# Hybrid SSD and GLA trunk on one core: sums of A beside the last scan, three kinds of work in the source's order, the meta state a piece apart

## The chip, the cores and the metric

The kernel runs on one core of a Trainium2 chip. The metric is the time of one execution on the device in microseconds, taken as the median of several runs. The engines are TensorE (PE: matrix products), VectorE (DVE) and GpSimd (POOL) for elementwise work, ScalarE (ACT: activations, copies, and a second queue of transfers) and SyncE (SP), whose queue issues most transfers and executes them in order: an issue that waits for a free tile holds all issues behind it.

## The reference, cut to what matters

One layer of a decoder trunk over 16 meta tokens and 2048 real ones, width 1024, all in float32:

```
u = rmsnorm(h, norm_w)
z, xbc, dt, q, k, v, g_gla, a_lr, merge_g = split(u @ w_in)
y_ssd = rmsnorm(ssd(silu(conv(xbc)), softplus(dt)) * silu(z))       # Mamba-2, 4 groups, chunks of 128
y_gla = rmsnorm(gla(q, k, v, log_sigmoid(a_lr @ w2 + b) / 16)) * silu(g_gla)   # 4 heads, chunks of 64
merged = sum over the two branches of sigmoid(merge_g) * (y @ w_branch)
out = rmsnorm(h + merged @ w_out, final_norm_w), without the meta tokens
```

Both scans carry a state from chunk to chunk and start from the state that the 16 meta tokens leave. The SSD scan multiplies its scores by decays exp(seg), seg being the difference of two running sums.

## The kernel before, in words

**Arithmetic.** Each fp32 operand is split into a high and a low half (ACT copies to the high half, DVE or POOL subtracts to get the low one), and `accum` (L185, L186, L187) makes each product of three matmuls.

**First phase.** The 2064 tokens go in four blocks of 512 (`BLK`); block 0 has the 16 meta tokens as well (`m0`). A block has eight units, four SSD (`ssd_proj`, `ssd_scan`) and four GLA (`gla_proj`, `gla_scan`). All of these are generators; `step()` advances the running ones by a piece after each piece of the projections, so that scans run a unit behind. Block 0 loads raw weights (`wr`, 3 tiles), splits them (L165 on ACT, L166 on POOL, into `whl`, 4 tiles) and saves the split ones by SP (L181); later blocks load those (L161). Beside the projections there run:

- `late_constants` (L332 on): the GLA gate's second matrix `gw2` in three loads (L335), its split, the masks (L339). It is called once, at the start of unit 1 of block 0.
- `fetch_u(b+1)` from unit 4 on: for each of four chunks the sum of squares of the rows of x (`rows_rstd`: two loads L258 and two squares L259, in `acc` tiles, of which there are two and which the convolution of the projections uses as well), then the normed columns (L294 loads, DVE and ACT form and split `u`).
- `beside_unit`: the differences of B that a Strassen product needs (`make_sums`: loads L76, POOL subtracts L80, stores from ACT's queue L83).

In `ssd_scan`, `before(c)` makes scores and decays of a chunk (L552: four Relu per chunk on ACT; then Exp L554, L555 masks on DVE), `after(c)` uses them (L564, L565 with the state `s_ssd`); `meta_state()` (L508 to L519) makes the state of the meta tokens first. `g_all` (L437) is the copy of a gate projection out of PSUM.

**Second phase.** Seven stages follow (gate, branch 0 and branch 1 for each half of the tokens, then out), each a 7-product Strassen form with products taken in the order 1, 2, 6, 7, 5, 3, 4. A `Stage` loads and splits B (`load_b` L884, `prep_b` L889 on ACT and L890 on DVE), loads A (`load_a` L896), makes its sums on POOL (`sum_a` L905 to L908), splits A (`prep_a` L914 on ACT, L915 on DVE, into a ring `aops` of 7) and multiplies (`product`). Products 1 and 2 need no sums of A; 6, 7, 5 and 3 do.

**The transition.** The table `between` does the first loads, splits and four early products (`NEARLY`; pairs 0 and 1, products 1 and 2) of the first gate stage beside the steps k = 0 to 8 of the last GLA scan, which ends with transposes (L803). Then the pools of the first phase are closed, new ones opened, and `run(-1)` does what the table `todo` has ahead of the next product.

**What sets the order.** In the first phase PE and SP run in the source's order; ACT, DVE and POOL run in the order of a scheduler's own simulation. In the stages only SP is held to the source's order.

Of the kernel before, what the change touches and what calls it, by code (L numbers as in the profile page):

```python
# [14 lines left out]
P = 128  # L15
# [25 lines left out]
def trunk_kernel(ctx: ExitStack, tc: tile.TileContext, xm, xmt, w_feat, w_tok, w_zm, w_br, w_o,  # L41
# [29 lines left out]

    def make_sums(pool, tag, nb, braw, sums, j, c, store):
        cs = slice(c * HB, (c + 1) * HB)
        pair = [mk(pool, [P, 512], F32, tag, bufs=nb).rearrange("p (i c) -> p i c", i=2) for _ in range(2)]
        for r, (k, t) in zip((t[:, i] for t in pair for i in range(2)), ((0, 1), (0, 0), (1, 1), (1, 0))):
            nc.sync.dma_start(r, braw(4 * k + j, t)[:, cs])  # L76
        yield
        (b12, b11), (b22, b21) = [(t[:, 0], t[:, 1]) for t in pair]
        for o, x, y in ((b11, b12, b11), (b12, b22, b12), (b22, b22, b11), (b21, b21, b22)):
            nc.gpsimd.tensor_tensor(o, x, y, op=ALU.subtract)  # L80
        yield
        for dst, src in zip(sums, pair):
            store.dma_start(dst[j][:, :, cs], src)  # L83

# [136 lines left out]
    def halves_of(pool, tag):  # L221

        bks = [bank(pool, tag) for _ in range(2)]
        return bks, [(i // 2, bks[i // 2][:, i % 2 * 256:(i % 2 + 1) * 256]) for i in range(4)]

    def rstd_of(ssq, n, scale):
        r = mk(sm, [P, 4], F32, "rstd")
        nc.vector.tensor_scalar(r[:, :n], ssq, scale, EPS, op0=ALU.mult, op1=ALU.add)
        nc.gpsimd.tensor_tensor(r[:, :n], r[:, :n], mhalf[:, :n], op=ALU.pow)
        return r  # L230
# [6 lines left out]
    def load_u(b):  # L237
# [6 lines left out]
        def rows_rstd(r0, n, vector=False):  # L244
# [9 lines left out]
            else:  # L254
                s2 = mk(sm, [P, 2], F32, "ss2")
                for i in range(2):
                    xt = mk(wk, [P, META + BLK], F32, "acc")[:, :BLK]
                    nc.sync.dma_start(xt, xm[r0:r0 + n, i * BLK:(i + 1) * BLK])  # L258
                    nc.scalar.activation(xt, xt, AF.Square, accum_out=s2[:, i:i + 1])  # L259
                nc.vector.tensor_tensor(ss, s2[:, 0:1], s2[:, 1:2], op=ALU.add)  # L260
# [6 lines left out]
        if m0:  # L267
            rm_s = rows_rstd(0, META, True)
        for c in range(NCH):
            rs.append(rows_rstd(META + b * BLK + c * P, P, c % 2))  # L270
            yield
# [15 lines left out]
        else:  # L287
# [3 lines left out]
            yield  # L291
        for kt in range(KT):
            xk = mk(wk, [P, META + BLK], F32, "act" if m0 else "acc", bufs=NACT if m0 else 2)[:, :tt]
            nc.sync.dma_start(xk, xmt[:, kt, row0:row0 + tt])  # L294
            for ps, a, n in rbs:
                nc.vector.scalar_tensor_tensor(xk[:, a:a + n], xk[:, a:a + n], norm_w[:, kt:kt + 1], ps[:, :n],
                                               op0=ALU.mult, op1=ALU.mult)
            nc.scalar.activation(uh[:, kt, :tt], xk, AF.Copy)
            nc.scalar.dma_start(u_left[b][kt], xk[:, m0:])
            nc.vector.tensor_tensor(ul[:, kt, :tt], xk, uh[:, kt, :tt].bitcast(F32), op=ALU.subtract)  # L300
            yield
        return uh, ul
# [29 lines left out]
    def late_constants():  # L332
        w2r = mk(wk, [P, META + BLK], F32, "acc")[:48, :512]
        for i in range(3):
# [159 lines left out]
    def ssd_scan(o, g, feats, zs):  # L494
# [37 lines left out]
        def before(c):  # L532
# [18 lines left out]
            for h in range(4):  # L551
                nc.scalar.activation(dm[:, h], cb[:, h], AF.Relu, scale=-1.0,  # L552
                                     bias=tkc[:, ci, 4 * g + h:4 * g + h + 1])
            nc.scalar.activation(dm, dm, AF.Exp, scale=-1.0)  # L554
            nc.vector.tensor_tensor(dm, dm, scm[:, c].unsqueeze(1).to_broadcast([P, 4, P]), op=ALU.mult)  # L555
# [27 lines left out]
        if m0:  # L583
            meta_state()
        for c in range(1, NCH):
            before(c)
            after(c - 1)
            yield
# [233 lines left out]
    def beside_unit(key):  # L822
        for j in range(4):
            for c in range(2):
                yield from make_sums(wpool, "wr", NWR, *sums[key], j, c, nc.scalar)
                yield
# [3 lines left out]
    for b in range(nblk):  # L830
        o = new_block(b, next_u[b])
        for i in range(SG + GH):
            if (b, i) in beside:
                begin(beside_unit(beside[b, i]))
            if (b, i) == (0, 1):
                late_constants()
            if i == 1:
                begin(gates(o))
            if i == SG and b + 1 < nblk:
                begin(fetch_u(b + 1))  # L840
            for _ in ssd_proj(o, i) if i < SG else gla_proj(o, i - SG):
                step()
        save(0)

# [16 lines left out]
    rpl = pool2("raws", 1)  # L861
    apl = pool2("aops", 7)
    
# [6 lines left out]
    class Stage:  # L870
# [8 lines left out]
        def load_b(self, p, j):  # L879
            src = {1: lambda j: self.braw(j, 0), 2: lambda j: self.braw(4 + j, 0), 3: lambda j: self.braw(4 + j, 1),  # L880
                   4: lambda j: self.sums[1][j][:, 1], 5: lambda j: self.sums[0][j][:, 1],
                   6: lambda j: self.sums[1][j][:, 0], 7: lambda j: self.sums[0][j][:, 0]}[p]
            raw = self.braws[p, j] = mk(rpl, [P, BLK], F32, "br", bufs=5)
            nc.sync.dma_start(raw, src(j))  # L884
# [33 lines left out]
        def product(self, n, p, early=False):  # L918
# [10 lines left out]
            if p in (1, 6, 5):  # L929
                sn = mk(rpl, [P, BLK], F32, "br", bufs=5) if early else mk(opl, [P, BLK], F32, "sn", bufs=6)  # L930
                nc.scalar.activation(sn, ps, AF.Copy)  # L931
                self.snap[n, p] = sn
# [60 lines left out]
    def out_stage():  # L993
        fns, res, ssq = [], {}, {}

        def fetch(n, i, t):
# [3 lines left out]
            if t and len(fns) < 2:  # L1000
                for hf in range(2):
                    fns.append(mk(rpl, [P, BLK], F32, "br", bufs=5))
                    nc.sync.dma_start(fns[hf], fnw[:, hf * BLK:(hf + 1) * BLK].to_broadcast([P, BLK]))
# [84 lines left out]
    def flush(due):  # L1088
# [124 lines left out]
```

## Time and profile before

| what | value |
| --- | --- |
| runs | 2352.01, 2353.92, 2355.6 us (median 2353.92) |
| profiled execution | 2356.45 us |
| its span | 2354.7 us |
| PE busy | 2252.8 us (96%), 12641 matmuls |
| DVE, ACT, POOL busy | 66%, 50%, 29% |
| DMA | 518.05 MB, mean 220 GB/s |

A row of a timeline has start, duration, engine, line, operation, output<-inputs and, in brackets, idle time before it and what ended that ("xN": N such operations follow one another). A row of waits reads "engine, its operation <- what it waited for: us in total, times, longest". A row of windows has the length, then busy us (and instructions) of PE, PE's weight loads, DVE, ACT and POOL, then the granted TensorE clock as a share of full speed, the DMA share and GB/s. Durations of neighbouring matmuls overlap, so their starts tell the pace: 0.228 us for one of 512 columns.

### The profile page before, as it was taken

How to read it: one execution, taken by the hardware profiler on the slowest of the kernel's cores; microseconds unless marked ns; L12 is line 12 of the kernel's file. 1: busy time of each engine (PE TensorE's matmuls, PEld its weight loads, DVE VectorE, ACT ScalarE, POOL GpSimd, SP SyncE). 2: the span in 40 equal slices, each digit the busy share in tenths (PEclk: the TensorE clock that was granted, in tenths of full speed). 3: DMA queues.
4: the chain of work that ended last, by engine and by line, in shares of the span. 5: the costliest groups of instructions: out<-in, count | busy, mean ns of one | idle time of the engine just before them, and what ended most of it. 6: DMA issues, size and time to landing. Idle time of an engine off the chain costs nothing.

```text
span 2354.7 us, 36479 instructions
## 1 busy us (share of the span) xinstructions
PE 2252.8 (96%) x12641; PEld 1956.3 (83%) x12641; DVE 1553.0 (66%) x2895; ACT 1183.3 (50%) x2758; POOL 679.4 (29%) x681
## 2 busy tenths in 40 slices
PE   7799999999999999999999999879999999999998
PEld 7689889889888988888988898758888878878786
DVE  5577665666576667566568655664578864778875
ACT  4565655455534455543456443554554444554543
POOL 3334433122311212221122200037423254413341
PEclk9899999999999999999999999989999999999999
DMA  7665875666886666787676655547577866777753
GB/s 270 216 209 180 301 243 186 207 218 212 265 269 201 209 220 215 241 259 225 194 227 217 206 169 161 171 146 237 193 236 269 293 230 202 256 259 255 254 165 116
DMA packets 301545, 518.05 MB, mean 220 GB/s; under 512 B 27696, under 2 KB 143664, under 8 KB 301360
## 3 DMA queue, kind: packets, MB, share of 16 engines
q1 hardware_dynamic: 200400, 402.84, 53.0%
q10 hardware_dynamic: 100960, 112.88, 13.9%
q8 instruction: 99, 1.62, 0.3%
q14 instruction: 86, 0.70, 0.1%
HBM read 368.42 MB, written 147.19 MB: 219 GB/s over the span
## 4 chain that ended last, share of the span: by engine, by line
PE 36%; DMA 6%; DVE 4%; issue 3%; ACT 2%; SPq 1%; POOL 0%; ACTq 0%; DVEq 0%; POOLq 0%
PE pj L187 8%; PE pj L185 8%; PE pj L186 8%; PE pt L187 2%; PE pt L185 2%; PE pt L186 2%; DMA br<-br_t 2%; DVE b L890 1%; PE pc L186 1%; PE pc L187 1%; PE pc L185 1%; DMA m<-io 1%; DVE a L915 1%; DMA br<-gate_t 1%; PE pc L698 1%
## 5 line engine op out<-in xcount | busy, mean ns | idle before, releaser
L185 PE MATMUL pj<-u,whl 128*128 128x512 f32 (+1 forms) x1184 | 447.2, 378 | 11.7 <-ACT g_all L437 3.6
L187 PE MATMUL pj<-u,whl 128*128 128x512 f32 (+1 forms) x1184 | 431.2, 364 | 0.8 <-POOL whl L166 0.8
L186 PE MATMUL pj<-u,whl 128*128 128x512 f32 (+1 forms) x1184 | 429.9, 363 | 0.0
L185 PE MATMUL pj<-whl,u 128*128 128x256 f32 (+1 forms) x992 | 290.8, 293 | 8.4 <-ACT whl L165 6.9
L187 PE MATMUL pj<-whl,u 128*128 128x256 f32 (+1 forms) x992 | 284.0, 286 | 1.5 <-DVE u L300 1.5
L186 PE MATMUL pj<-whl,u 128*128 128x256 f32 (+1 forms) x992 | 284.1, 286 | 1.1 <-POOL whl L166 1.1
L185 PEld LDWEIGHTS pj<-u,whl 128*128 128x128 f32 x1184 | 225.4, 190 | 49.7 <-ACT g_all L437 4.0
L185 PE MATMUL pj<-b,a 128*128 128x512 f32 x640 | 253.1, 399 | 11.5 <-ACT sn L931 6.8
L187 PE MATMUL pj<-b,a 128*128 128x512 f32 x640 | 252.9, 395 | 5.9 <-DVE a L915 5.9
L187 PEld LDWEIGHTS pj<-u,whl 128*128 128x128 f32 x1184 | 224.7, 190 | 36.8 <-POOL whl L166 1.1
L186 PEld LDWEIGHTS pj<-u,whl 128*128 128x128 f32 x1184 | 225.4, 190 | 33.5
L186 PE MATMUL pj<-b,a 128*128 128x512 f32 x640 | 251.6, 393 | 0.0
L185 PEld LDWEIGHTS pj<-whl,u 128*128 128x128 f32 x992 | 191.7, 193 | 9.6 <-ACT whl L165 7.1
L890 DVE TENSOR_TENSOR b<-br,b 128x512 fp32r<-128x512 f32 x196 | 160.0, 839 | 51.5 <-ACT b L889 51.2
L186 PEld LDWEIGHTS pj<-whl,u 128*128 128x128 f32 x992 | 191.7, 193 | 2.1 <-POOL whl L166 1.7
L187 PEld LDWEIGHTS pj<-whl,u 128*128 128x128 f32 x992 | 191.5, 193 | 2.2 <-DVE u L300 2.2
L80 POOL TENSOR_TENSOR wr<-wr 128x256 f32<-128x256 f32 x80 | 67.5, 843 | 428.3 <-DMA wr<-y 173.2
L166 POOL TENSOR_TENSOR whl<-wr,whl 128x512 fp32r<-128x512 f32 (+1 forms) x100 | 131.7, 1323 | 188.5 <-ACT whl L165 154.8
L889 ACT ACTIVATE b<-br 128x512 fp32r<-128x512 f32 x196 | 119.3, 627 | 112.9 <-DMA br<-br_t 43.4
L905 POOL TENSOR_TENSOR as<-ar,ar 128x512 f32<-128x512 f32 x40 | 56.4, 1410 | 414.7 <-DMA ar<-in_w_br 174.8
L915 DVE TENSOR_TENSOR a<-ar,a 128x512 fp32r<-128x512 f32 x160 | 131.3, 835 | 65.3 <-ACT a L914 62.2
L479 DVE SCALAR_TENSOR_TENSOR acc<-cin,hcw,acc 128x512 f32<-128x512 f32 (+1 forms) x192 | 154.5, 805 | 27.1 <-ACT acc L475 26.6
(274 smaller groups left out, 5057.3 us busy)
## 6 DMA issues: line engine op xcount, KB each, us to landing
whl<-k_s SPq DMA_DIRECT2D x96, 512.0 KB, 4.5
whl<-k_g SPq DMA_DIRECT2D x96, 512.0 KB, 4.1
whl<-k_v SPq DMA_DIRECT2D x48, 512.0 KB, 3.8
whl<-k_z SPq DMA_DIRECT2D x36, 512.0 KB, 3.7
wr<-in_w_feat SPq DMA_DIRECT2D x64, 256.0 KB, 4.4
k_s<-whl SPq DMA_DIRECT2D x32, 512.0 KB, 3.6
cb<-cumd ACTq DMA_DIRECT2D x64, 256.0 KB, 5.3
y<-gg ACTq DMA_DIRECT2D x64, 256.0 KB, 4.5
```

The source lines that it names most:

```text
L80: nc.gpsimd.tensor_tensor(o, x, y, op=ALU.subtract)
L166: nc.gpsimd.tensor_tensor(hl[:, 1], raw, hl[:, 0].bitcast(F32), op=ALU.subtract)
L185: nc.tensor.matmul(ps, sh, mh, start=first, stop=False, **kw)
L186: nc.tensor.matmul(ps, sh, ml, start=False, stop=False, **kw)
L187: nc.tensor.matmul(ps, sl, mh, start=False, stop=last, **kw)
L479: nc.vector.scalar_tensor_tensor(acc, cin[:, k:k + tt], hcw[:, ti, k:k + 1], acc, op0=ALU.mult, op1=ALU.add)
L698: nc.tensor.matmul(ps[:, r * P:(r + 1) * P], kq[:, 2 * r * P:(2 * r + 1) * P], kq[:, (2 * r + 1) * P:(2 * r + 2) * P], start=True, stop=True)
L889: nc.scalar.activation(t[:, 0], raw, AF.Copy)
L890: nc.vector.tensor_tensor(t[:, 1], raw, t[:, 0].bitcast(F32), op=ALU.subtract)
L905: nc.gpsimd.tensor_tensor(s1, a21, a22, op=ALU.add)
L915: nc.vector.tensor_tensor(t[:, 1], src, t[:, 0].bitcast(F32), op=ALU.subtract)
```

## The change

1. `late_constants` is called in unit 0 of block 0, after its second piece, and its raw tile is of the `act` ring (8 tiles) instead of `acc`.
2. `meta_state()` of each SSD scan in block 0 is followed by a yield, so the rest of the scan's first piece comes a piece later.
3. `in_order(...)` (keep_in_program_order) holds three kinds of ACT operations behind the ACT operation traced before them: the decays, the stores of B's sums, the row squares of `fetch_u`.
4. `rows_rstd` is a generator: both loads, a yield, both squares. Columns are loaded a piece ahead.
5. Transition: B of the early products is loaded and split two tiles at a time from a ring of its own (`br0`, 2 tiles); the later `br` ring of 5 lies in a pool that is opened after the first phase is closed. `sum_a(0)` and `sum_a(1)` are called in steps 6 and 8 of `between`. The `aops` ring has 6 tiles instead of 7. An early snapshot takes an `as` tile instead of a `br` tile.

The diff, cut:

```
-            store.dma_start(dst[j][:, :, cs], src)
+            order(store.dma_start(dst[j][:, :, cs], src))
...
+    in_order = tc.keep_in_program_order
...
-                for i in range(2):
-                    xt = mk(wk, [P, META + BLK], F32, "acc")[:, :BLK]
+                xts = [mk(wk, [P, META + BLK], F32, "acc")[:, :BLK] for _ in range(2)]
+                for i, xt in enumerate(xts):
                     nc.sync.dma_start(xt, xm[r0:r0 + n, i * BLK:(i + 1) * BLK])
-                    nc.scalar.activation(xt, xt, AF.Square, accum_out=s2[:, i:i + 1])
+                yield
+                for i, xt in enumerate(xts):
+                    in_order(nc.scalar.activation(xt, xt, AF.Square, accum_out=s2[:, i:i + 1]))
...
+        def column(kt):
             xk = mk(wk, [P, META + BLK], F32, "act" if m0 else "acc", bufs=NACT if m0 else 2)[:, :tt]
             nc.sync.dma_start(xk, xmt[:, kt, row0:row0 + tt])
+            return xk
+        xk = column(0)
+        if not m0:
+            yield
+        for kt in range(KT):
...
+            if kt + 1 < KT:
+                xk = column(kt + 1)
...
-        w2r = mk(wk, [P, META + BLK], F32, "acc")[:48, :512]
+        w2r = mk(wk, [P, META + BLK], F32, "act", bufs=NACT)[:48, :512]
...
-                nc.scalar.activation(dm[:, h], cb[:, h], AF.Relu, scale=-1.0,
-                                     bias=tkc[:, ci, 4 * g + h:4 * g + h + 1])
-            nc.scalar.activation(dm, dm, AF.Exp, scale=-1.0)
+                in_order(nc.scalar.activation(dm[:, h], cb[:, h], AF.Relu, scale=-1.0,
+                                              bias=tkc[:, ci, 4 * g + h:4 * g + h + 1]))
+            in_order(nc.scalar.activation(dm, dm, AF.Exp, scale=-1.0))
...
         if m0:
             meta_state()
+            yield
...
-                yield from make_sums(wpool, "wr", NWR, *sums[key], j, c, nc.scalar)
+                yield from make_sums(wpool, "wr", NWR, *sums[key], j, c, nc.scalar, in_order)
...
-            if (b, i) == (0, 1):
-                late_constants()
...
-            for _ in ssd_proj(o, i) if i < SG else gla_proj(o, i - SG):
+            for n, _ in enumerate(ssd_proj(o, i) if i < SG else gla_proj(o, i - SG)):
                 step()
+                if (b, i, n) == (0, 0, 1):
+                    late_constants()
...
-    apl = pool2("aops", 7)
+    apl = pool2("aops", 6)
+    bt_raws = {"early": (rpl, "br0", 2)}
...
-            raw = self.braws[p, j] = mk(rpl, [P, BLK], F32, "br", bufs=5)
+            pool, tag, nb = bt_raws.get("all") or bt_raws["early"]
+            raw = self.braws[p, j] = mk(pool, [P, BLK], F32, tag, bufs=nb)
...
-            s1, s2, s4 = [mk(spl, [P, 4, P], F32, "as", bufs=6) for _ in range(3)]
+            s1, s2, s4 = [mk(rpl, [P, 4, P], F32, "as", bufs=6) for _ in range(3)]
...
-        if p == 1:
-            at(i - LOAD + (n % 2), lambda st=st, n=n, i=i: st.sum_a(n) if i < NEARLY else load_sum_a(st, n))
+        if p == 1 and i >= NEARLY:
+            at(i - LOAD + (n % 2), lambda st=st, n=n: load_sum_a(st, n))
...
+    def b_ops(p, js):
+        for j in js:
+            st.load_b(p, j)
+            st.prep_b(p, j)
     between = {
-        0: [lambda: [st.load_b(1, j) for j in range(4)], lambda: st.load_a(0)],
-        1: [lambda: [st.prep_b(1, j) for j in range(4)], lambda: st.prep_a(0, 1)],
-        2: [lambda: [st.load_b(2, j) for j in range(4)], lambda: st.load_a(1)],
-        3: [lambda: st.product(0, 1, True), lambda: [st.prep_b(2, j) for j in range(4)], lambda: st.prep_a(0, 2)],
+        0: [lambda: st.load_a(0), lambda: b_ops(1, (0, 1))],
+        1: [lambda: b_ops(1, (2, 3)), lambda: st.prep_a(0, 1)],
+        2: [lambda: st.load_a(1), lambda: b_ops(2, (0, 1))],
+        3: [lambda: st.product(0, 1, True), lambda: b_ops(2, (2, 3)), lambda: st.prep_a(0, 2)],
...
-        6: [lambda: flush(stores[:]), lambda: stores.clear(), lambda: st.product(1, 1, True)],
+        6: [lambda: flush(stores[:]), lambda: stores.clear(), lambda: st.product(1, 1, True), lambda: st.sum_a(0)],
...
-        8: [lambda: flush(stores[:]), lambda: stores.clear()],
+        8: [lambda: flush(stores[:]), lambda: stores.clear(), lambda: st.sum_a(1)],
...
+    bt_raws["all"] = opl, "br", 5
```

Lines shift by the change: L258 and L259 become L260 and L263, L335 L348, L437 L450, L552 becomes L565, L564 and L565 L577 and L578, L803 L817, L889 and L890 L905 and L906, L905 to L908 L921 to L924, L914 and L915 L930 and L931.

SP's queue before, from the end of unit 0 to the start of unit 1 (`gw` is the gate's second matrix, `cmsk` the masks, `k_s` a saved split weight):

```order
L181 DMA k_s_1_718<-whl_712 128x1024
L175 DMA wr_847<-in_w_feat 128x512
L181 DMA k_s_0_773<-whl_767 128x1024
L175 DMA wr_878<-in_w_feat 128x512
L335 DMA acc_921<-in_gw 16x512 x3
L339 DMA tok_103_927<-in_cmsk 128x896
L181 DMA k_s_1_804<-whl_798 128x1024
L175 DMA wr_935<-in_w_tok 128x512
```

The same loads in SP's queue after, now in unit 0:

```order
L175 DMA wr_517<-in_w_zm 128x288
L181 DMA k_zm_477<-whl_471 256x1x288
L175 DMA wr_524<-in_w_zm 128x288
L348 DMA act_589<-in_gw 16x512 x3
L352 DMA tok_63_595<-in_cmsk 128x896
L181 DMA k_zm_484<-whl_478 256x1x288
L175 DMA wr_602<-in_w_feat 128x512
```

The four constants' loads moved from behind the feature weights of unit 0 to ahead of the first of them.

PE before, in the first SSD scan of block 0 (L517 makes the meta tokens' state):

```order
L187 MATMUL pj_1134<-u_253,whl_1166 128x264
L517 MATMUL pc_1211<-c_120_1081,bt_1083 128x256
L540 MATMUL pt_1216<-cst,act_664 128x128
L540 MATMUL pt_1216<-cst,act_754 128x128
L540 MATMUL pt_1216<-cst,act_840 128x128
L564 MATMUL pc_1234<-c_128_1100,sq_1107 128x64 x4
L565 MATMUL pc_1234<-s_ssd,act_918 128x256
```

PE there after, the first rows of it:

```order
L187 MATMUL pj_1134<-u_253,whl_1166 128x264
L530 MATMUL pc_1211<-c_120_1081,bt_1083 128x256
L185 MATMUL pj_1220<-u_253,whl_1222 128x264
...
L187 MATMUL pj_1221<-u_253,whl_1253 128x264
L553 MATMUL pt_1300<-cst,act_673 128x128
...
L577 MATMUL pc_1318<-c_128_1100,sq_1107 128x64 x4
L578 MATMUL pc_1318<-s_ssd,act_927 128x256
```

Between the meta state and the scan's transposes there now stand 48 matmuls of the projections (the first and last are shown).

POOL before, from the end of the last scan (`rstd`) to the sums of A (`as`, `ar`):

```order
L229 TENSOR_TENSOR rstd_17226<-rstd_17226,mhalf 128x4
L229 TENSOR_TENSOR rstd_17461<-rstd_17461,mhalf 128x4
L905 TENSOR_TENSOR as_17510<-ar_17088,ar_17090 128x512
...
L908 TENSOR_TENSOR as_17512<-ar_17092,as_17511 128x512
L905 TENSOR_TENSOR as_17517<-ar_17220,ar_17222 128x512
...
L908 TENSOR_TENSOR as_17519<-ar_17224,as_17518 128x512
```

POOL there after:

```order
L231 TENSOR_TENSOR rstd_17228<-rstd_17228,mhalf 128x4
L921 TENSOR_TENSOR as_17395<-ar_17080,ar_17082 128x512
...
L924 TENSOR_TENSOR as_17397<-ar_17084,as_17396 128x512
L921 TENSOR_TENSOR as_17468<-ar_17212,ar_17214 128x512
...
L924 TENSOR_TENSOR as_17470<-ar_17216,as_17469 128x512
L231 TENSOR_TENSOR rstd_17475<-rstd_17475,mhalf 128x4
```

The eight sums of the first two pairs moved from behind the scan's last `rstd` to ahead of it.

More of the change, by code (lines that the diff above doesn't have):

```diff
@@ L70, in trunk_kernel, with make_sums @@
     nsb = seq // UNIT
-    def make_sums(pool, tag, nb, braw, sums, j, c, store):
+    def make_sums(pool, tag, nb, braw, sums, j, c, store, order=lambda ins: ins):
         cs = slice(c * HB, (c + 1) * HB)
@@ L267, in load_u @@
         if m0:
-            rm_s = rows_rstd(0, META, True)
+            rm_s = yield from rows_rstd(0, META, True)
         for c in range(NCH):
-            rs.append(rows_rstd(META + b * BLK + c * P, P, c % 2))
+            r = yield from rows_rstd(META + b * BLK + c * P, P, c % 2)
+            rs.append(r)
             yield
@@ L291, in load_u @@
             yield
-        for kt in range(KT):
+        def column(kt):
             xk = mk(wk, [P, META + BLK], F32, "act" if m0 else "acc", bufs=NACT if m0 else 2)[:, :tt]
             nc.sync.dma_start(xk, xmt[:, kt, row0:row0 + tt])
+            return xk
[3 more added lines that the diff above has]
+        for kt in range(KT):
             for ps, a, n in rbs:
@@ L929, in product @@
             if p in (1, 6, 5):
-                sn = mk(rpl, [P, BLK], F32, "br", bufs=5) if early else mk(opl, [P, BLK], F32, "sn", bufs=6)
+                sn = mk(rpl, [P, 4, P], F32, "as", bufs=6).rearrange("p k c -> p (k c)") if early else mk(opl, [P, BLK], F32, "sn", bufs=6)
                 nc.scalar.activation(sn, ps, AF.Copy)
@@ L1001, in fetch @@
                 for hf in range(2):
-                    fns.append(mk(rpl, [P, BLK], F32, "br", bufs=5))
+                    fns.append(mk(opl, [P, BLK], F32, "br", bufs=5))
                     nc.sync.dma_start(fns[hf], fnw[:, hf * BLK:(hf + 1) * BLK].to_broadcast([P, BLK]))
```

## The prediction

> **What bounds the kernel now.** I read the page's busy shares first, then TensorE's waits over the whole span, then the waits, timelines and windows of the places where the change acts.
>
> ```profile
> PE 2252.8 (96%) x12641; PEld 1956.3 (83%) x12641; DVE 1553.0 (66%) x2895; ACT 1183.3 (50%) x2758; POOL 679.4 (29%) x681
> PE   7799999999999999999999999879999999999998
> ```
>
> TensorE (PE) is busy 96% of 2354.7 us and no other engine over 66%. Only two places dip under 9 tenths, the first 120 us and slices 26 to 27 (about 1530 to 1590 us, the end of the scans). No matmul is removed, so only PE's idle time and slow clock can be won. The answer on PE's waits (total us, times, longest us) gives the idle time:
>
> ```profile
> PE pj L185 <- ACT whl L165: 10.2, 2, 6.9
> PE pj L187 <- DVE a L915: 5.9, 2, 4.5
> PE pc L565 <- DVE s_ssd L519: 4.8, 1, 4.8
> PE pc L564 <- DVE sq L555: 4.6, 3, 2.5
> PE pj L185 <- ACT a L914: 4.6, 1, 4.6
> PE pj L185 <- ACT g_all L437: 3.6, 2, 3.4
> PE pj L185 <- DMA whl<-k_g: 2.8, 2, 1.7
> ```
>
> These seven sum to 36.5 us, nearly all in single waits. Each belongs to one part of the change; the parts are priced in turn.
>
> **A, late constants.** Traced after unit 0, their load takes one of two `acc` tiles that the convolution holds. SP, in source order, stands behind it:
>
> ```profile
> SPq L335 <- DVE act L483: 15.8, 1, 15.8
> 60.48 1.25 SPq L335 DMA_DIRECT2D acc<-in_gw  x3
> PE pj L185 <- ACT whl L165: 6.9, 1, 6.9
> PE pj L186 <- POOL whl L166: 1.1, 2, 0.8
> 70.00:80.00 10.00, 9.73 (x68) 9.25 (x69) 0.00 (x0) 2.20 (x4) 4.70 (x4) 0.82 0.94 323
> ```
>
> SP issues nothing for 15.8 us until 60.48, so the next weights come late and PE waits 6.9 + 1.1 us (both rows are those of 56 to 82 us). The window row's last three numbers are granted clock, DMA share and GB/s: 0.82 after the wait, which costs 10 x 0.18 = 1.8 us. Afterwards the tile is from the `act` ring, still free at 26 us, and SP does not stop. I take all: -8.0 and -1.8. If the queue is late anyway (DMA share 0.94 just after), half returns; zero is the other end.
>
> It has a price at the start. ACT's new order puts the split of the first feature weight behind the copies of the last `zm` results, which need PE's last `zm` matmul.
>
> ```profile
> 32.40 0.63 ACT L165 ACTIVATE whl<-wr 128x512 fp32r<-128x512 f32 x1 [3.65 <-DMA wr<-in_w_feat]
> 34.65 0.37 PE L185 MATMUL pj<-u,whl 128*128 128x264 f32 x1
> 34.76 0.21 ACT L375 ACTIVATE alr<-pj 128x48 f32<-128x48 f32 x1
> L166 POOL TENSOR_TENSOR whl<-wr,whl 128x512 fp32r<-128x512 f32 (+1 forms) x100 | 131.7, 1323 | 188.5 <-ACT whl L165 154.8
> ```
>
> Before, the split ran at 32.40 and PE went on at 34.65 without a wait. After, the split can start only when PE is through with `zm`: three small copies ahead of it (0.21 each), 0.63 on ACT, then 1.32 on POOL for the low half: +2.6. Ends: 0, if the copies run early and the first matmuls need only the high half for long enough, and +4.3, with 1.7 us more because four more issues, 0.42 us each (1.25 for three in the L335 row), now stand on SP ahead of that weight's load.
>
> **B, meta state a piece apart.** PE's L540, L564 and L565 followed directly on L517; now 48 projection matmuls stand between.
>
> ```profile
> 86.41 0.29 PE L186 MATMUL pj<-u,whl 128*128 128x264 f32 x1
> 86.53 0.28 PE L187 MATMUL pj<-u,whl 128*128 128x264 f32 x1
> 100.00:110.00 10.00, 5.80 (x31) 5.44 (x32) 9.02 (x23) 2.68 (x10) 2.24 (x3) 0.66 0.47 158
> ```
>
> At 0.12 us from start to start these are 5.8 us of cover for a wait of 4.8. The clock of 0.66 costs 5.80 x 0.34 = 2.0; 1.7 of it I put down to this wait. -4.8 - 1.7 = -6.5; ends 0, if DVE is as late again (it is busy 9.02 of 10 us there), and -6.8. Each first-block SSD scan has a piece more; it ends later beside projections that do not need it, so nothing.
>
> **C, decays in program order.** ACT ran decays (L552) ahead of `g_all`, the copy that empties a PSUM bank for PE:
>
> ```profile
> 88.18 0.97 ACT L552 ACTIVATE sq<-cb,tkc 128x128 f32<-128x128 f32 x3
> 89.73 0.46 ACT L437 ACTIVATE g_all<-pj,pv 128x264 f32<-128x264 f32 x1
> 90.24 0.39 PE L185 MATMUL pj<-u,whl 128*128 128x264 f32 x1 [3.42 <-ACT g_all L437]
> 90.00:94.00 4.00, 3.76 (x18) 3.76 (x19) 1.78 (x3) 3.83 (x11) 0.00 (x0) 0.57 0.90 269
> ACT sq L554 <- POOL wr L80: 14.2, 7, 2.6
> ```
>
> PE waited 3.42 us, then ran four microseconds at 0.57: 4 x 0.43 = 1.7 us. Together 5.1. The pins order decays among themselves, not against every copy; I take half, -2.5 (ends -5.1 and 0). The Trainium skill ("TensorE: Matmul & The Clock Gate", Part 1, What's actually happening) says that one idle window of about 3.4 us halves the clock until some 3.4 us of activity have passed; by that rule this wait costs 3.4/2 = 1.7 us more, and the trace agrees (0.57). By the same rule a wait shortened below about 3.4 us would win its clock term whole: the part would be -3.4 instead of -2.5 if half the wait stays.
>
> Later, the L564 waits (4.6 us, three) follow decays that stood on ACT behind sums' stores that wait for POOL (last row) and behind row squares that wait for loads. With stores and squares at the source's place: -3.0; ends -4.6 and +4, if a pinned operation holds ACT as long.
>
> **D, the transition.** Sums of A and the A operands of products 6, 7, 5 now come beside the last scan.
>
> ```profile
> L890 DVE TENSOR_TENSOR b<-br,b x8: 679/682/692, 1517.4 to 1528.6; 128x512 fp32r<-128x512 f32 x8
> 1563.49 0.80 PE L185 MATMUL pj<-b,a 128*128 128x512 f32 x1 [4.55 <-ACT a L914]
> 1569.18 0.80 PE L187 MATMUL pj<-b,a 128*128 128x512 f32 x1 [4.48 <-DVE a L915]
> 1555.14 1.01 POOL L229 TENSOR_TENSOR rstd<-rstd,mhalf 128x4 f32<-128x4 f32 x1 [21.04 <-DVE rstd L228]
> br<-gate_t SPq DMA_DIRECT2D x32, 256.0 KB, 3.8
> L890 DVE TENSOR_TENSOR b<-br,b x9: 676/893/1786, 1560.9 to 1570.9; 128x512 fp32r<-128x512 f32 x9
> 1560.00:1570.00 10.00, 2.04 (x4) 1.22 (x5) 9.13 (x8) 5.40 (x10) 7.90 (x5) 0.50 0.53 167
> 1570.00:1580.00 10.00, 10.00 (x34) 7.93 (x34) 10.00 (x18) 9.35 (x18) 0.00 (x0) 0.73 0.69 219
> ```
>
> Idle 4.55 + 4.48, clock 2.04 x 0.5 + 10 x 0.27 = 3.7: 12.7 us. POOL is idle 21 us before its last rstd, so the eight adds fit there. What is late next is B: its tiles now come from a pool that opens after the last transpose (1563.49 - 4.55 = 1558.94), so a load (3.8 us from issue to landing) and a split of 0.63 put the first product 4.4 us behind it, and with 1.7 us of clock (half of today's, for half the idle time) the transition costs 6.1. That wins 6.6. Against it, two A preps of some 0.6 us each stand on ACT ahead of the last scan step, +0.9 of 1.2. And the early B tiles have two buffers where there were five: four rounds of 3.8 + 0.63 + 0.68 are 20 us where the eight tiles took 11 (first L890 row), so the last comes 9 us later; scan matmuls stand between, and I take +2.0 for the early product (0, 2). Net -3.7. Ends: -9 (nothing lost beside the scan, clock term gone too) and +3 (load at twice the time, preps wholly and the early B by 5 on the path).
>
> **E, row prefetch.** Both `acc` loads of a row are now issued in one piece, and the second waits for the tile that the unit's fourth channel holds.
>
> ```profile
> 621.67 0.85 SPq L161 DMA_DIRECT2D whl<-k_g  x2
> 625.67 0.69 DVE L483 SCALAR_TENSOR_TENSOR act<-act,acc 128x512 f32<-128x512 f32 x1 [0.17 <-ACT act L482]
> ACT acc L259 <- DMA acc<-in_xm: 3.2, 1, 3.2
> PE pj L185 <- ACT whl L165: 3.3, 1, 3.3
> ```
>
> SP went on to the weights at 621.67; now it passes behind that L483. ACT no longer stands 3.2 us for the load in mid-convolution, so L483 comes near 623: about 1.8 us later than 621.67. PE already waited for these weights in all three prefetching blocks (1.1 and 1.7, whose sum is the `k_g` row, and 3.3 in the first, last row), with no slack, so +1.8, +1.6, +1.8 = +5.2. Ends: -6.1 (later rows hold SP less, all three go) and +13 (L483 as late as now, 625.67 + 0.7 - 621.67 = 4.7 each, less 1).
>
> **Nothing.** The operand ring of 6 instead of 7 still leaves each A prep five products of cover; its price is the first rival. The column loads of the prefetch go one piece earlier on SP, and the work between is the projections' own. Early snapshots move from a `br` to an `as` tile, whose six are free before the first sum.
>
> **Sum:** -8.0 - 1.8 + 2.6 - 6.5 - 2.5 - 3.0 - 3.7 + 5.2 = -17.7 us. The profiled execution took 2356.45 us, 2.5 above the median of the runs (2353.92): 2338.8 by the one, 2336.2 by the other; I take 2337, since the runs to come will be medians and this profile lies high among them.
>
> **Rivals.**
> Slower: the smaller ring. Each A prep then waits for one product later, 12 matmuls of 0.228, or 2.7 us.
>
> ```profile
> ACT a L914 <- PE pt L187: 33.7, 25, 2.1
> PE pj L187 <- DVE a L915: 1.4, 1, 1.4
> ```
>
> ACT already waits for a product to free an operand buffer 25 times (first row, 160 preps in all). If each of these waits grows by 1 us of its 2.7 and PE inherits it, the kernel takes 2337 + 25 = 2362; it decides from 16.9 / 25 = 0.68 us each, and the loss is measurable from 0.86. Against it: PE waited for these preps 1.4 us in all of 1580 to 2300 us (second row), so they have run well ahead.
>
> Transition and prefetch eat more: D gives nothing, E doubles: 2337 + 3.7 + 5.2 = 2345.9. The mechanism for D: POOL's adds slow the scan's DVE. Beside POOL the median of L890 is 893 ns and the longest 1786, where it is 682 without POOL (the two L890 rows); some 10 us of adds then cost DVE 10 / 7.9 x (9.13 - 8 x 0.68) = 4.7 us (window 1560 to 1570: 7.90 POOL, 9.13 for 8 on DVE), on a scan whose DVE steps PE waits for. The Trainium skill ("GPSIMD Engine Reference", Specifications) has POOL's SBUF ports shared with VectorE and contended by two-input operations, which is this case.
>
> Better: no start price, no prefetch cost, decays whole: 2337 - 2.6 - 5.2 - 2.6 = 2326.6. For it speaks that squares of later rows no longer hold the tiles that SP waits for; against it, that PE had no slack at the three weights.
>
> No change: the change only moves waits. The split at the start comes late enough to hold back the queue that the early constants were to free, and meta's state meets a DVE that is busy 9.02 of 10 us, so that A's 9.8 and B's 6.5 come to nothing: 2353.3. Against it, nothing on SP waits near 26 us for a tile that is held.
>
> **Chances.** Forecast (2329 to 2343, D and E at the inner halves of their ends) 0.53, transition and prefetch 0.21, better 0.09, no change 0.10, slower 0.07. 0.2% is 4.7 us, about what a measurement tells from nothing: faster 0.83, same 0.10, slower 0.07. The range 2322 to 2350 takes in the first three and leaves out the last two.
>
> **What would show it.** A: no L335-type SP wait, PE without 6.9 at 61 us, a wait of 2 to 3 near 35 us. B: no 4.8 near 100 us. C: `g_all` wait under 2 us. D: 4 to 5 us between the last transpose and the first product, no L914 wait. E: waits for `k_g` weights of near 3 us in blocks 1 and 2. Wrong: many small waits for `a` after 1580 us, or SP waits over 10 us on other lines.

## The result, and the profile after

The changed kernel takes 2508.21 us (median of five runs, 2500.6 to 2512.13) where the kernel before takes 2353.92: a ratio of 1.0654, 95% interval 1.0626 to 1.0681. It is 154 us slower; 2337 was forecast, with an upper end of 2350. The page of the changed kernel, busy shares and PE's slices:

```profile
span 2498.8 us, 36430 instructions
PE 2294.1 (92%) x12641; PEld 1989.7 (80%) x12641; DVE 1543.1 (62%) x2895; ACT 1195.8 (48%) x2758; POOL 676.7 (27%) x681
PE   7899899978879998887999889988999999999998
```

The same 12641 matmuls take 41.3 us more of busy time (2294.1 against 2252.8), at a mean granted clock of 0.960 instead of 0.985, and the dips now run through the first phase (slices 1 to 24) instead of standing at its two ends; slices 27 and 28 are the transition. PE's waits in the changed kernel, the five largest sums:

```profile
PE pj L185 <- DMA whl<-k_g: 41.5, 8, 9.7
PE pj L185 <- DMA whl<-k_z: 41.1, 7, 9.2
PE pj L185 <- DMA whl<-k_s: 18.0, 6, 3.6
PE pj L185 <- ACT whl L165: 16.3, 5, 6.1
PE pc L577 <- DVE sq L568: 11.8, 9, 2.4
```

PE waits 100.6 us for split weights on their way from memory (first three rows); before it was 2.8 us for `k_g` and none for `k_z` and `k_s`. What held the weights is on SP, in the changed kernel's waits of that queue:

```profile
SPq L76 <- DMA br_t<-wr: 133.8, 12, 22.3
SPq L76 <- DMA gate_t<-wr: 117.4, 11, 20.8
SPq L76 <- DMA out_t<-wr: 92.4, 7, 20.8
SPq L260 <- ACT acc L263: 91.5, 14, 17.2
```

SP stands 343.6 us in 30 waits at L76, the load for the next difference of B, until the store of an earlier one (`br_t<-wr` and so on) has left a `wr` tile, and 91.5 us at the row loads until a row square has left an `acc` tile. Before, no wait of L76 was for a `wr` store, and the row loads (then L258) stood 29.5 us for squares.

One such chain in the changed kernel, from the timelines of POOL, ACT, SP and PE, and the clock in windows about it:

```profile
600.70 0.90 POOL L80 TENSOR_TENSOR wr<-wr 128x256 f32<-128x256 f32 x1 [2.17 <-DMA wr<-in_w_o]
608.44 0.63 ACT L495 ACTIVATE act<-acc 128x512 f32<-128x512 f32 x1 [3.62 <-DVE acc L492]
608.44 1.19 ACTq L83 DMA_DIRECT2D out_t<-wr  x2
596.39 15.41 SPq L76 DMA_DIRECT2D wr<-in_w_o  x4
611.89 0.86 SPq L161 DMA_DIRECT2D whl<-k_z  x2
616.13 0.58 PE L185 MATMUL pj<-whl,u 128*128 128x256 f32 x1 [5.12 <-DMA whl<-k_z]
616.00:620.00 4.00, 3.87 (x18) 3.87 (x19) 0.00 (x0) 0.00 (x0) 0.00 (x0) 0.51 0.74 295
620.00:624.00 4.00, 4.00 (x36) 4.00 (x36) 0.69 (x1) 0.74 (x2) 0.00 (x0) 1.00 0.00 0
```

POOL has finished the difference at 601.6. Its store is held behind the convolution's L495, which ACT cannot run before 608.44, since DVE is late with `acc`. SP's four loads at L76, begun at 596.39, end at 611.8 and only then the weights `k_z` are issued; PE stands 5.12 us for them and then runs four microseconds at a granted clock of 0.51. The Trainium skill ("TensorE: Matmul & The Clock Gate", Part 1, What's actually happening) has the clock at half after an idle window of about 3.4 us, until about 3.4 us of sustained work have passed. This row agrees. From the one trace to the other (spans of 2354.7 and 2498.8 us) PE's idle time grows by 102.8 us and its busy time by 41.3, which together make the 144.1 us.

Where the time goes along the program is seen from the start of the n-th matmul of line L185 (3496 in each trace), after less before:

```
start before (us)   86    172    245    328   535    683    897   1134   1261   1405   1545   2230   2324
difference (us)    -3.8  -12.0  -10.0   +8.9  +14.0  +64.2  +70.1 +117.8 +121.1 +147.3 +150.8 +137.2 +143.7
```

At 172 and 245 us the changed kernel is 12 and 10 us ahead, where A, B and the `g_all` half of C had forecast 16.2. The loss comes in the units in which sums or row squares run beside the projections: from 549 to 747 us of the changed kernel, for one, SP stands 122 us for them. From 1405 us on, the transition and the second phase together win 3.6 us in this trace; the part on D shows what stands behind that small number.

### The profile page after: what moved, and what is told of

It is laid out like the page before. It is cut to its first block, busy times and chain, and to the rows that moved or that the text cites. A ratio compares the mean times of both kernels' runs of the same rounds, so it can differ in the third digit from the quotient of the medians.

```text
span 2498.8 us, 36430 instructions
## 1 busy us (share of the span) xinstructions
PE 2294.1 (92%) x12641; PEld 1989.7 (80%) x12641; DVE 1543.1 (62%) x2895; ACT 1195.8 (48%) x2758; POOL 676.7 (27%) x681
## 4 chain that ended last, share of the span: by engine, by line
PE 66%; DMA 14%; DVE 9%; issue 4%; ACT 4%; POOL 2%; SPq 1%; ACTq 0%; DVEq 0%; POOLq 0%
PE pj L185 16%; PE pj L187 15%; PE pj L186 15%; PE pt L185 3%; PE pt L187 3%; PE pt L186 2%; DMA whl<-k_g 2%; PE pc L185 1%; PE pc L186 1%; DVE acc L492 1%; PE pc L187 1%; PE pc L712 1%; PE pc L577 1%; DMA whl<-k_z 1%; DMA whl<-k_s 1%
## 5 line engine op out<-in xcount | busy, mean ns | idle before, releaser
L185 PE MATMUL pj<-u,whl 128*128 128x512 f32 (+1 forms) x1184 | 457.1, 386 | 82.3 <-DMA whl<-k_g 41.5
L187 PE MATMUL pj<-u,whl 128*128 128x512 f32 (+1 forms) x1184 | 440.6, 372 | 2.9 <-POOL whl L166 2.1
L186 PE MATMUL pj<-u,whl 128*128 128x512 f32 (+1 forms) x1184 | 440.0, 372 | 0.0
L185 PE MATMUL pj<-whl,u 128*128 128x256 f32 (+1 forms) x992 | 299.2, 302 | 50.8 <-DMA whl<-k_z 41.1
L185 PEld LDWEIGHTS pj<-u,whl 128*128 128x128 f32 x1184 | 232.7, 197 | 128.6 <-DMA whl<-k_g 45.1
L186 PE MATMUL pj<-whl,u 128*128 128x256 f32 (+1 forms) x992 | 290.4, 293 | 1.1 <-POOL whl L166 1.1
L187 PE MATMUL pj<-whl,u 128*128 128x256 f32 (+1 forms) x992 | 289.8, 292 | 1.6 <-DVE u L311 1.6
L187 PEld LDWEIGHTS pj<-u,whl 128*128 128x128 f32 x1184 | 231.5, 196 | 41.6 <-POOL whl L166 4.2
L185 PE MATMUL pj<-b,a 128*128 128x512 f32 x640 | 254.6, 398 | 10.9 <-ACT sn L947 6.2
L186 PEld LDWEIGHTS pj<-u,whl 128*128 128x128 f32 x1184 | 232.7, 197 | 34.4
L185 PEld LDWEIGHTS pj<-whl,u 128*128 128x128 f32 x992 | 198.2, 200 | 55.7 <-DMA whl<-k_z 42.7
L186 PEld LDWEIGHTS pj<-whl,u 128*128 128x128 f32 x992 | 198.5, 200 | 2.1 <-POOL whl L166 1.7
L187 PEld LDWEIGHTS pj<-whl,u 128*128 128x128 f32 x992 | 198.0, 200 | 2.3 <-DVE u L311 2.3
L906 DVE TENSOR_TENSOR b<-br,b 128x512 fp32r<-128x512 f32 x196 | 153.3, 802 | 46.9 <-ACT b L905 46.3
L905 ACT ACTIVATE b<-br 128x512 fp32r<-128x512 f32 x196 | 120.0, 627 | 108.4 <-DMA br<-br_t 34.1
L921 POOL TENSOR_TENSOR as<-ar,ar 128x512 f32<-128x512 f32 x40 | 59.4, 1485 | 411.9 <-DMA ar<-in_w_br 131.1
L931 DVE TENSOR_TENSOR a<-ar,a 128x512 fp32r<-128x512 f32 x160 | 130.6, 823 | 65.1 <-ACT a L930 60.9
```

The lines of the kernel that those rows point to most:

```text
L185: nc.tensor.matmul(ps, sh, mh, start=first, stop=False, **kw)
L186: nc.tensor.matmul(ps, sh, ml, start=False, stop=False, **kw)
L187: nc.tensor.matmul(ps, sl, mh, start=False, stop=last, **kw)
L905: nc.scalar.activation(t[:, 0], raw, AF.Copy)
L906: nc.vector.tensor_tensor(t[:, 1], raw, t[:, 0].bitcast(F32), op=ALU.subtract)
L931: nc.vector.tensor_tensor(t[:, 1], src, t[:, 0].bitcast(F32), op=ALU.subtract)
```

## The experiments

Theories: **S**, the pinned stores keep `wr` tiles and SP stands before the weights; **R**, the row prefetch does the same with `acc` tiles; **D**, the pinned decays delay ACT's copies (in this section D is this theory, not the prediction's part D, the transition). Each ratio is against runs of the kernel before on the same chip in the same job (its medians there: 2350.1, 2352.5, 2351.4, 2352.8). Differences in us are between medians, some of them from different jobs, so they carry a few us of doubt.

**Store pin off.**

```
-  yield from make_sums(wpool, "wr", NWR, *sums[key], j, c, nc.scalar, in_order)
+  yield from make_sums(wpool, "wr", NWR, *sums[key], j, c, nc.scalar)
```

> The changed kernel with one pin taken off: the stores of B's sums (L83) are again placed on ACT by the scheduler; decays and row squares stay pinned, all else stays as changed. Theory S (stores): pinned, a store stands on ACT behind convolution work that waits for PE, the wr tile comes free late, SP stands at the next L76 load and the weights behind it reach PE late; SP waits 343 us for such tiles after and about 32 before. Then L76 waits fall below 60 us and the time falls by at least 100 us, to 2360 to 2400. Theory R (row prefetch: both loads in one piece and pinned squares hold SP at L260): the time stays above 2450. Theory D (the pinned decays delay ACT's other copies): also above 2450.

2401.84 us, ratio 1.0216 (1.0189 to 1.0243): 106.4 us of the loss are gone, and no wait of L76 on a `wr` store is left. S holds for two thirds. What stays on SP and PE in this run:

```profile
SPq L260 <- ACT acc L263: 98.5, 14, 16.3
PE pj L185 <- DMA whl<-k_g: 16.9, 4, 6.5
PE pj L185 <- ACT whl L165: 15.5, 5, 5.4
```

**Row prefetch as before** (stores and decays still pinned).

```
-  xts = [two acc tiles]; both loads; yield; in_order(both squares)
+  for i in range(2): acc tile; load; nc.scalar.activation(... AF.Square ...)
   (columns: loaded in the piece that uses them)
```

> The changed kernel with fetch_u as before: load, square, load, square in one piece without a pin, columns loaded in their own piece. Theory R: SP waits at L260 (113 us after, 50 before) go, and the time falls by over 100 us to about 2380. Theory S: only the part of the prefetching units falls, 10 to 40 us, to 2460 to 2495, with L76 waits still above 250 us. Theory D: no change, 2490 to 2512.

2466.67 us, 1.0488 (1.046 to 1.0517): 41.5 us less, a little beyond what S allowed and far from R's 2380. R is a second cause, not the first.

**Decays unpinned** (stores and squares still pinned).

```
-  in_order(nc.scalar.activation(dm[:, h], cb[:, h], AF.Relu, ...)) ... in_order(... AF.Exp ...)
+  nc.scalar.activation(dm[:, h], cb[:, h], AF.Relu, ...) ... nc.scalar.activation(dm, dm, AF.Exp, scale=-1.0)
```

> The changed kernel with the decays (L565, L567) unpinned; stores and squares stay pinned. Theory D: time falls by over 100 us. Theories S and R: 2480 to 2520, within 1% of the changed kernel, the g_all wait of 3 us comes back; the pinned store has fewer pinned ACT operations ahead of it, so it may also gain some.

2537.78 us, 1.0796 (1.0764 to 1.0828): 29.6 us slower than the changed kernel, which no theory expected. Under pinned stores the decays' pin helps. The traces show where the loss lies: SP stands 375.3 us at L76 instead of 343.6, PE waits 31.9 us for `k_s` instead of 18.0 and 12.2 us for the scan's state `s_ssd` where there was no such wait, and its busy time grows by 14.3 us; the 11.8 us for `sq` go. Why the stores come still later was not isolated.

**Store pin alone, on the kernel before.**

```
-  store.dma_start(dst[j][:, :, cs], src)
+  tc.keep_in_program_order(store.dma_start(dst[j][:, :, cs], src))     # beside the projections only
```

> The kernel before with one thing added: the stores of B's sums held to the source's order on ACT. Theory S: slower by 80 to 150 us, 2430 to 2500, with SP waits at L76 of some 300 us. Theories R and D: within 10 us of 2354.

2528.12 us, 1.0756 (1.0725 to 1.0787): one pin makes a larger loss than the whole change. SP's waits in it:

```profile
SPq L76 <- DMA br_t<-wr: 152.0, 12, 26.0
SPq L76 <- DMA gate_t<-wr: 141.4, 11, 27.5
SPq L76 <- DMA out_t<-wr: 102.2, 7, 27.2
SPq L258 <- ACT acc L259: 21.6, 12, 3.6
```

395.6 us at L76, and the row loads stand no longer than before. S by itself is shown; R and D have no part in this run.

**Is it SP's queue, or ACT's delay?** The changed kernel, its sums loaded from another queue.

```
-  nc.sync.dma_start(r, braw(4 * k + j, t)[:, cs])
+  (nc.gpsimd if tag == "wr" else nc.sync).dma_start(r, braw(4 * k + j, t)[:, cs])
```

> The changed kernel with all three pins, but the loads of B's sums (L76) are issued from GpSimd's queue instead of SP's. The stores still come late and the wr tiles with them, yet no weight load stands behind a load that waits for one. Theory S in its full form (the harm is SP's queue standing, not the late sums themselves): waits for k_z, k_g, k_s of about 100 us in sum fall to under 30 and the time to 2390 to 2430 (what is left is the row prefetch). Rival (the pinned stores hurt by delaying ACT, whatever queue loads): stays above 2470.

2422.41 us, 1.0297 (1.0278 to 1.0317). The stores are still late: GpSimd's queue now stands 270.9 us for them in 44 waits at L76. Yet 85.8 us of 106.4 come back once no weight load stands behind L76. PE's and SP's waits there:

```profile
PE pj L185 <- DMA whl<-k_g: 32.5, 6, 9.0
PE pj L185 <- ACT whl L165: 15.3, 5, 5.3
SPq L260 <- ACT acc L263: 145.5, 18, 19.9
```

PE's waits for `k_z` and `k_s` are gone. The sum did not quite fall under 30 as expected: the `k_g` weights belong to the GLA units, where the row loads hold SP, 145.5 us now instead of 91.5. What the other 20.6 us are was not isolated.

**What in the row prefetch?** Free stores, squares unpinned, both loads still in one piece.

```
-  in_order(nc.scalar.activation(xt, xt, AF.Square, accum_out=s2[:, i:i + 1]))
+  nc.scalar.activation(xt, xt, AF.Square, accum_out=s2[:, i:i + 1])
```

> The run with free stores (2401.8) with the squares of the rows unpinned as well, both loads of a row still in one piece. If the pin of the squares is what the row prefetch costs (51 us between free stores and s_base): 2352 to 2365, with SP waits at L260 near 50 us instead of 141. Rival, the prediction's E (the second load waits for the tile of the fourth channel): still 2385 to 2402.

2350.03 us, 0.9991 (0.9975 to 1.0006): with the stores free, the squares' pin costs 51.8 us; two loads in one piece cost nothing that is seen here. SP and ACT in block 0 show how, in the run with free stores and pinned squares:

```profile
228.51 0.33 SPq L175 DMA_DIRECT2D wr<-in_w_tok  x1
241.96 0.94 SPq L260 DMA_DIRECT2D acc<-in_xm  x2
239.22 0.28 ACT L562 ACTIVATE bt<-pt 128x128 f32<-128x128 f32 x1 [1.96 <-DVE tok L559]
240.69 0.63 ACT L567 ACTIVATE sq<-sq 128x512 f32<-128x512 f32 x1
241.23 0.62 ACT L263 ACTIVATE acc<-acc 128x512 f32<-128x512 f32 x1
```

The first pair of rows was issued by 220 us and has long landed (3.1 us median). Its squares stand behind a decay (L567) of the scan, that one behind a copy (L562) that waits for DVE. SP stands at the next pair from 228.8 to 241.96, and no weight is issued.

**All but stores and rows** (s_base: store pin off and rows as before), and on it three parts undone one at a time.

> The changed kernel with the store pin off and fetch_u as before; early constants, meta state a piece apart, pinned decays and the new transition stay. If the whole loss is stores plus row prefetch, as the theory now says, the four other parts show what they bring: 2350.1 - 14 (lead over the kernel before at 200 us in the run with free stores) - 2 (transition and stages) = 2334, within 2325 to 2345. Rival: what is left also costs in blocks 1 to 3 (pinned decays); then 2355 to 2375.

2351.41 us, 0.9997 (0.9985 to 1.0009): no faster than before, and between the two ranges. The trace is 18.0 us ahead of the kernel before at 328 us and 1.2 us behind it at 1261, so the rival of a cost in later blocks has the kind right, and put it too large.

```
s_trans_old:  the second phase from its pools on as before (sums of A behind the scan, br and aops rings)
```

> The same as s_base with the second phase from the pools on as before: sums of A after the scan, br and aops rings as before. The prediction's D said that the new transition wins 3.7 us: then this is 3.7 us slower than s_base. Rival (read off the traces, where the new transition lost about 2 us and the stages won about 10, the out stage lost 7): within 2 us of s_base.

2355.69 us, 1.0009 (0.9997 to 1.002): the intervals overlap; not decided.

```
s_late_old:
-  if (b, i, n) == (0, 0, 1): late_constants()      # raw tile "act"
+  if (b, i) == (0, 1): late_constants()            # raw tile "acc"
```

> The same as s_base with late_constants back at unit 1 in an acc tile. The prediction's A: -8.0 - 1.8 + 2.6 = -7.2, so 7.2 us slower than s_base. Rival: the stall at the start (7 us by the alignment of the changed kernel) takes most of it: within 3 us.

2356.35 us, 1.0022 (1.0007 to 1.0038): 5 us slower than s_base, the intervals just touching.

```
s_meta_old:
-  meta_state(); yield
+  meta_state()
```

> The same as s_base without the yield behind meta_state. The prediction's B: 6.5 us slower than s_base. Rival: the wait only moves to the next chunk of the scan: within 2 us.

2353.65 us, 1.0003 (0.9992 to 1.0014): not told from s_base.

**The decays again**, now without the stores' pin: s_base with decays unpinned.

> s_base (no store pin, rows as before) with the decays unpinned too. The prediction's C: 5.5 us slower than s_base. Rival, from s_base's trace, where the L568 wait for the masked decays grew from 4.6 us in three to 10.4 in ten: the pins cost as much as they win; within 3 us of s_base, or faster by up to 10, with the g_all wait of 3.4 back.

2335.92 us, 0.9929 (0.9913 to 0.9945): 15.5 us faster than s_base, more than either expectation allowed. A decay in s_base, from the timelines of ACT and PE, and PE's wait over the span:

```profile
503.26 0.28 ACT L553 ACTIVATE bt<-pt 128x128 f32<-128x128 f32 x1 [2.57 <-DVE tok L550]
503.43 1.27 ACT L556 ACTIVATE sq<-cb,tkc 128x128 f32<-128x128 f32 x4
506.47 1.81 PE L568 MATMUL pc<-c,sq 128*128 128x64 f32 x8 [1.82 <-DVE sq L559]
PE pc L568 <- DVE sq L559: 10.4, 10, 2.4
```

ACT idles 2.57 us for the operand of the copy L553; the decays L556 behind it need only `cb` and `tkc`, and PE pays 1.82 us. With the pin off, all of the scan's decays have run before 490 us, the wait is 1.9 us in two, and between 490 and 512 us PE has no wait at all. Of the 19.6 us between the two traces this wait is 8.5, and 11.0 are PE's busy time.

**The parts that win, alone and together.** s_best is the kernel before with only the early constants and the yield behind `meta_state`; the other two have one of these each.

> Only the early constants and the yield behind meta_state of the whole change: no pins, rows and second phase as before. By the alignment of s_base and s_trans_old, which led by 18 to 21 us at the end of the first block and lost 13 to 15 of it in the SSD scans of later blocks, where the decays are pinned: 2352.5 - 14 = 2338, if the pins lost it. Rival (whatever puts the scans later loses it): 2347 to 2355.

> The kernel before with only the early constants. The prediction's A: -7.2 us, so 2345. Rival (alignment of s_late_old and s_base, 7 us apart at 86 us and 11 at 172): -10 or more, under 2342.

> The kernel before with only the yield behind meta_state. The prediction's B: -6.5 us, so 2346. Rival: with s_best at 2332.4 and A at 7 to 11, B is 8 to 12. Rival below (s_meta_old against s_base): -2.

s_best 2332.43 us, 0.9922 (0.9902 to 0.9942), beats both kernels. Early constants alone: 2344.32, 0.9962 (0.995 to 0.9974), or -8.5 us. The yield alone: 2343.36, 0.9952 (0.9938 to 0.9966), or -9.4 us. By sum -17.9, together -18.9.

**The whole change without its three pins.**

> The whole change without its three pins: early constants, meta state a piece apart, both loads of a row in one piece with columns ahead, new transition. If the pins are the whole loss: with stores and squares free 2350.0, less 15.5 for the decays (s_base to s_decay_free) = 2334.5, within 2328 to 2342. Rival (each pin's price depends on the others, as decays pinned won 30 us under the pinned stores): 2343 to 2360.

2334.36 us, 0.9918 (0.9905 to 0.993), where 2334.5 was expected. The pins are the whole loss.

**Stores from GpSimd's queue**, on s_best (`nc.scalar` becomes `nc.gpsimd` in `beside_unit`).

> s_best with the stores of B's sums issued from GpSimd's queue, right behind its subtractions, so that ACT does not stand for them. If ACT's stands (some 49 us in 17 waits on L80 for wr tiles in s_best's ACT waits) reach PE at all: 2 to 8 us faster than s_best (2332). Rival: they are hidden, or the issue costs GpSimd as much: within 2 us, or slower if GpSimd's queue issues late.

2341.15 us, 0.9946 (0.9933 to 0.996): no gain, if anything a loss. Either ACT's stands for these stores were hidden before, or the issues cost GpSimd as much as they spare ACT; the run does not part the two.

## Why the prediction was wrong, step by step

**The step that failed** is the second half of C: "With stores and squares at the source's place: -3.0; ends -4.6 and +4, if a pinned operation holds ACT as long." It rests on the first half of C, that the pins "order decays among themselves, not against every copy": in the traces a pinned operation stands behind whatever ACT operation was traced ahead of it, the store behind L495, the squares behind a decay. And it priced a pin by how long ACT itself would stand. It did not ask which tile a late store or square keeps, who waits for that tile, and what is queued behind the waiter. Taken off one after the other, the pins measured 106.4 us (stores), 51.8 (squares) and 15.7 (decays, 2350.03 to 2334.36): 173.9 where -5.5 was written for C with its decays. These prices are not constants: the stores' pin costs 178 us on the kernel before, and the decays' pin saves 29.6 while the stores are pinned. The same view of the profile that A was read from, SP standing at a load for a held tile, should have been turned on every operation that frees a tile of SP's. None of the rivals named it. The slower one was the ring of 6, and between 1720 and 2480 us PE has no wait for `a`. The better one, and E's lower end, had it the other way round: later rows were to hold SP less, and the wait for the squares grew from 29.5 to 91.5 us. Of its two signs of being wrong the second, SP waits over 10 us on other lines, is what came: up to 22.3 us at L76.

**A** was right: -7.2 forecast, -8.5 measured. In the trace with only this part PE no longer waits for the weights at 61 us, and at the start it waits 1.6 and 0.8 us, 2.4 where 2.6 was put. In the changed kernel a third wait follows these two:

```profile
36.66 0.39 PE L185 MATMUL pj<-u,whl 128*128 128x264 f32 x1 [1.61 <-ACT whl L165]
38.01 0.39 PE L187 MATMUL pj<-u,whl 128*128 128x264 f32 x1 [0.84 <-DVE dw L395]
47.12 0.59 PE L185 MATMUL pj<-u,whl 128*128 128x264 f32 x1 [2.00 <-ACT acc L488]
```

The trace with this part alone has no wait for `acc` over 0.7 us there, and that without pins has none, so the third wait is not the early constants' by themselves.

**B** had its wait right: in the trace with only this part the 4.8 us at 100 us are gone. The total, -6.5 forecast and -9.4 measured, agrees better than its parts do: a wait of 4.2 us for `acc` comes in their place, and waits for `whl`, `tok` and `gg` in block 0 shrink by 3.3, 2.9 and 2.1 us. None of these was in the forecast, so part of the agreement is luck. And on s_base, among pinned decays, the same part is worth 2.2 us, not told from zero.

**C's decays** won at `g_all` what was said: the longest wait fell from 3.42 to 2.12 us, and the clock behind it stayed at 1.00, so that 1.3 us of wait and the 1.7 of clock went, 3.0 where 2.5 was put. They lost more elsewhere: +15.5 instead of -2.5, by the mechanism of s_base's rows above. That pinned operations wait for what stands ahead of them was named only as an end of the range.

**D** (-3.7) is not told from zero: s_best and s_decay_free, with the old and the new second phase, are 0.9922 and 0.9929; s_trans_old and s_base go the other way (1.0009 and 0.9997). In the changed kernel's transition (1680 to 1720 us) PE waits

```profile
PE pc L712 <- DVE c L719: 5.3, 1, 5.3
PE pj L185 <- ACT b L905: 4.7, 2, 4.5
PE pt L817 <- ACT ot L812: 3.8, 1, 3.8
```

The waits for `a` went, and the wait for B came, 4.7 us, as forecast (4.4). New is 5.3 us inside the scan, for DVE. In s_base it falls together with the first sum on POOL:

```profile
1531.12 3.17 POOL L912 TENSOR_TENSOR as<-ar,ar 128x512 f32<-128x512 f32 x1
1533.41 1.03 DVE L695 TENSOR_TENSOR sq<-sq,act 128x128 f32<-128x128 f32 x1
1539.93 1.22 PE L703 MATMUL pc<-sq 128*128 128x128 f32 x4 [5.33 <-DVE c L710]
```

That L695 takes 1.03 us where two of them took 0.49 earlier. This is the rival of POOL's adds slowing the scan, in size too (4.7 us was put); that the adds are its cause was not isolated.

The gain of the transition is there all the same, and is lost again near the end. From 1405 to 2230 us of the kernel before, the eleven traces with the new second phase win 6.4 to 11.4 us on it, and from 2230 to 2324 they lose 4.9 to 9.1; the six other traces with the old one differ from it by at most 3.6 in the first stretch and not at all in the second. In the second stretch, the out stage, PE has no wait in the seven with the old phase, and 2.8 to 6.5 us of waits for a copy `sn` in all eleven others. In s_decay_free the longest is

```profile
2212.25 0.34 ACTq L1097 DMA_DIRECT2D out_h<-io  x1
2212.64 0.60 ACT L938 ACTIVATE sn<-pj 128x512 f32<-128x512 f32 x1 [6.31 <-DVE io L1029]
2213.29 0.79 PE L185 MATMUL pj<-b,a 128*128 128x512 f32 x1 [5.20 <-ACT sn L938]
```

ACT stands 6.31 us for `io`, which the store of the output needs, and the copy that PE waits for comes behind that store. D's sum had no term for the out stage. Which of D's edits changed the order there was not isolated.

**E** (+5.2) did not come: without any pin, the rows as before give 2335.92 (s_decay_free) and the new ones 2334.36 (a_no_pins), where PE waits 2.4 us for `k_g` (2.8 in the kernel before). That the second load waits for the fourth channel's tile was the wrong wait. The tile that SP waited for was the square's.

Two readings beside the sum were off as well: the first rival counts 160 A preps in all, and L914 ran 280 times; and PE's last slice dips to 8 too. No term rests on either.

## What to carry to other kernels

Price a held order by the tiles that the held operation frees, not by the engine that it holds: follow tile to waiter to the queue behind the waiter, above all where one in-order queue carries both the operand loads that the bound engine lives on and loads that wait for a side task. A store that must be timely is not to be put behind work that waits for the bound engine. And test an edit's parts one by one: here two parts of a change that lost 154 us win 19 by themselves.

## What the runs showed of the hardware that was not expected

A run of waits costs more than its length: 102.8 us more of idle time came with 41.3 us more of busy time for the same matmuls. The wait need not be as long as the 3.4 us that the prediction put. First the run with the yield alone, then the changed kernel, each the wait for `g_all` and a window behind it:

```profile
88.16 0.39 PE L185 MATMUL pj<-u,whl 128*128 128x264 f32 x1 [3.10 <-ACT g_all L441]
89.50:92.90 3.40, 3.40 (x18) 3.40 (x17) 0.69 (x1) 3.40 (x8) 0.00 (x0) 0.50 0.93 309
85.11 0.39 PE L185 MATMUL pj<-u,whl 128*128 128x264 f32 x1 [2.12 <-ACT g_all L450]
85.00:89.00 4.00, 3.89 (x32) 3.89 (x33) 0.69 (x1) 3.95 (x7) 0.00 (x0) 1.00 0.86 254
```

After 3.10 us the clock was 0.50, after 2.12 us it was 1.00.

In these traces the issue of a store takes GpSimd longer than it takes ACT, by the rows on L83 in s_best_poolq and in s_best (durations in ns, min/median/max):

```profile
L83 POOL DMA_DIRECT2D gate_t<-wr x32: 665/682/948, 601.3 to 1307.9; - x32
L83 ACTq DMA_DIRECT2D gate_t<-wr x32: 520/521/543, 596.6 to 1302.0; - x32
```
